# Prompt latent attention with keys on partitions: row maxima as a 97th query feature, no transposes of exponentials

## Chip, cores and metric

One core of one Trainium2 chip. The metric is device time in microseconds (us) of one execution of the whole program; lower is better. The engines are TensorE (PE; its weight loads are listed as PEld), VectorE (DVE), ScalarE (ACT), GpSimd (POOL) and SyncE (SP, which issues the DMAs). L177 is line 177 of the kernel file.

## What is computed

Two layers of a streaming encoder for 1024 prompt tokens and, with the same weights, 32 later sample tokens; model width 1024. In each layer three groups of heads work side by side: retention (4 heads), latent attention (8 heads, in the code `mla`) and a band attention (4 heads). Their outputs, times a gate, are concatenated and projected back. The change touches the prompt's latent attention alone:

```python
def _mla_prompt_attn(q, k, v):          # q, k: 96 features (64 normed + 32 rotated), v: 64
    scale = dq ** -0.5
    key_chunk = jnp.arange(S) // CHUNK   # CHUNK = 64
    def one_block(args):                 # a block of 128 queries
        q_chunk = (b_idx * Q_BLOCK + jnp.arange(Q_BLOCK)) // CHUNK
        s = jnp.einsum('bqhd,bkhd->bhqk', q_blk, k) * scale
        s = jnp.where(key_chunk[None, :] <= q_chunk[:, None], s, NEG_INF)
        p = jax.nn.softmax(s, axis=-1)
        return jnp.einsum('bhqk,bkhd->bqhd', p, v)
mix = jnp.concatenate([ret_o * silu(a_g), mla_o * silu(b_g), band_o * silu(c_g)], -1)
y = x + jnp.einsum('bte,ed->btd', mix, w_out)
```

## The kernel before

All of it is one program, written by the class `Kern`. Tokens are 9 tiles: 8 of 128 prompt tokens and one with the 32 of the sample. A product that needs more precision than the rounded type float32r gives is split in a high and a low part and takes three PE instructions: high times high, high times low, low times high.

`run` (L1526) goes through the layers. `layer_in` (L1431) makes the input projections in steps and spawns tasks: retention, band attention, the sample, and `mla_pair` (L784) for the first pair of heads. `mla_pair` loads queries, keys and values of two heads from DRAM (`sk`, `sq`, `sv`), transposes queries and keys on PE and writes their high and low parts to `self.sets` (in the trace `H`), with the 96 features on partitions.

Then `run` iterates over `mla(l)` (L821), which goes through units: 4 pairs of heads `hp`, 8 query tiles `b`, 2 heads `i` of the pair. A unit has three steps:

- `score` (L825): the scores of 128 queries (on partitions) with the `128 * (b + 1)` keys up to their own tile, in two pieces above 512. Three products a piece, then the masked corner, a row maximum on DVE, and on ACT the exponential, with the negated maximum as its bias and the sum of each row as second output. The exponentials are called `P`.
- `turn`, one unit later (`LAG_T`): `transposed` (L1204) turns each 128x128 block of `P` on PE by a product with the identity, so that keys come to partitions, and copies it out of PSUM (`PT`).
- `value`, two units later (`LAG_V`): for both heads of the pair, `pv` (L863) multiplies each `PT` block with the values of its key tile. Head 0 fills output rows 0 to 63 and head 1 rows 64 to 127: `self.mm(o[64 * i:64 * i + 64], vk[:, 64 * i:64 * i + 64], at[i][k], ...)` (in `values`, L1216). `inverse_rows` (L1231) brings the inverse sums to the features' layout by one more transpose (`rep`), and the result goes into `mix`.

Between the units `run` puts pieces of the output projection `out_part` (L1382), at rates set by `RATES`, `STARTS` and `OUT_PAGES`. The second of its two calls, with feature tiles that hold the latent heads, starts a token tile when `self.full` says that the last pair of heads is done for it; `pv` sets it to `b + 1`.

The order in which Python emits all this comes from the tasks (`poll`, `press`, `drive`, with rough prices per instruction); a scheduler then sets the final order on each engine. PSUM has 8 banks: 3 named `ps`, 3 `s`, 2 `pj`. SBUF has 60 pages of 128x512 float32.

Of the kernel before, what the change touches and what calls it, by code (L numbers as in the profile page):

```python
# [35 lines left out]
RATES = (0.45, 0.4, 0.8)  # L36
SMALL = 4
STARTS = (2, 40)
OUT_PAGES = (14, 20)
# [12 lines left out]
LAG_T, LAG_V = 1, 2  # L52
MLA_ORDER = "stv"
PAIR_AT = 2
# [3 lines left out]
NEED = dict(prep=4, misc=2, b=10, ret=4, bk=2, bq=7, band=12, smp=3, mla=4)  # L58
# [32 lines left out]
class Task:  # L91
    """A foreground task: its pages held, and whether and when it can go on."""
# [6 lines left out]
class Kern:  # L99
# [19 lines left out]
    # ---- storage  # L119
# [44 lines left out]
    # ---- instructions, each with its rough price for the emission order  # L164
# [87 lines left out]
    # ---- order of emission: background products, foreground tasks where they are ready  # L252
# [3 lines left out]
    def safe(self, k, task=None):  # L256
        """Whether the started tasks can still end, one after the other, when k pages are taken (by task)."""
# [65 lines left out]
    # ---- constants  # L323
    def setup(self):
# [4 lines left out]
        nc.vector.memset(self.ones, 1.0)  # L329
        self.nhalf = cp.tile([128, 16], F32, name="nhalf")  # L330
# [14 lines left out]
        self.G = cp.tile([128, 256], F32, name="G")  # L345
# [34 lines left out]
    def load_layer(self, l):  # L380
        A = self.A
        G = A["gains"]
        self.load(self.G, bass.AP(tensor=G.tensor, offset=G.offset + l * 256, ap=[[0, 128], [1, 256]]))
# [3 lines left out]
        self.ts(self.gret, self.cols[:, 2:4], 0.5, None, OP.mult)  # L387
        for j in range(2):
# [3 lines left out]

    def load_bias(self, l):
        """8 (bias - the bias of far keys) of the last 256 keys, masked, rows by query."""
# [87 lines left out]
    def first_prep(self, t, hT):  # L482
        """The first layer takes its input as it is, turned by the layout; its products are scaled by the rows' norms."""
# [40 lines left out]
    # ---- products of all tokens with one chunk of columns  # L524
# [19 lines left out]
    def stacked(self, p, ws, fts=range(8)):  # L544
        """Sample rows: high parts' products on rows 0-31, low parts' on 32-63 (64-95 only fill the array)."""
# [5 lines left out]
    def unload(self, t, p, W, z=None):  # L551
        """A chunk's product of token tile t in SBUF."""
# [13 lines left out]
    # ---- latent attention: queries, keys and values of a token tile  # L566
# [58 lines left out]
    def rope(self, x, cos, sin, tmp, out, H, half, n, eng, first="G"):  # L625
        """x, out: [n, H, 2, half]; tmp as x; cos, sin: [n, half] or [n, 2, half]."""
# [11 lines left out]
    def latent(self, p, ch, cl, ws):  # L638
        """Products of latents; without cl, ch holds high parts in columns 0-31 and low parts in 32-63."""
# [180 lines left out]

    def mla(self, l):  # L821
        sets = self.sets
        P, sums, PT = {}, {}, {}

        def score(hp, i, b):  # L825
            hs = sets[(2 * hp + i) % 4]
            nk = 128 * (b + 1)
            if nk <= 512:
                halves = [(0, nk)]
            else:  # L830
                a = 128 * ((b + 2) // 2)
                halves = [(0, a), (a, nk)]
            q = slice(128 * b, 128 * b + 128)
            m = self.st(2)
            pss = []
            for j, (a, e) in enumerate(halves):
                s = self.bank((e - a,), "pj" if self.spare and (j if len(halves) == 2 else i) else "s")
                self.mm(s, hs[:96, 2, q], hs[:96, 0, a:e], True, False)
                self.mm(s, hs[:96, 2, q], hs[:96, 1, a:e], False, False)
                self.mm(s, hs[:96, 3, q], hs[:96, 0, a:e], False, True)  # L840
                if e == nk:
                    self.memset(s[0:64, e - a - 64:e - a], NEG)
                self.red(m[:, j:j + 1], s, OP.max, negate=True)
                pss.append(s)
            bias = self.st(1)
            if len(halves) == 2:
                self.ts(bias, m[:, 0:1], m[:, 1:2], MLA_SCALE, OP.min, OP.mult)
            else:
                self.ts(bias, m[:, 0:1], MLA_SCALE, None, OP.mult)
            if not i:  # L850
# [800 lines left out]
```

## Time and profile before

| | |
|---|---|
| three runs | 1393.87, 1394.78 (median), 1399.46 us |
| profiled execution, span | 1392.4 us, 28787 instructions |
| PE busy | 1357.6 us (98%) |
| DVE busy | 864.9 us (62%) |
| ACT busy | 765.8 us (55%) |
| POOL busy | 457.8 us (33%) |
| DMA | 130.57 MB, mean 94 GB/s |

The profiled execution has no other time of its own than its span; the median of the three runs is 2.4 us above it. Busy time of PE is from instructions that overlap each other, since matmuls are pipelined. "a <- b" in a row of instructions is output from inputs; in a row of waits it is the waiting instruction and what released it.

### The profile page before, as it was taken

How to read it: one execution, taken by the hardware profiler on the slowest of the kernel's cores; microseconds unless marked ns; L12 is line 12 of the kernel's file. 1: busy time of each engine (PE TensorE's matmuls, PEld its weight loads, DVE VectorE, ACT ScalarE, POOL GpSimd, SP SyncE). 2: the span in 40 equal slices, each digit the busy share in tenths (PEclk: the TensorE clock that was granted, in tenths of full speed). 3: DMA queues.
4: the chain of work that ended last, by engine and by line, in shares of the span. 5: the costliest groups of instructions: out<-in, count | busy, mean ns of one | idle time of the engine just before them, and what ended most of it. 6: DMA issues, size and time to landing. Idle time of an engine off the chain costs nothing.

```text
span 1392.4 us, 28787 instructions
## 1 busy us (share of the span) xinstructions
PE 1357.6 (98%) x10339; PEld 1222.2 (88%) x10339; DVE 864.9 (62%) x2745; ACT 765.8 (55%) x2190; POOL 457.8 (33%) x682
## 2 busy tenths in 40 slices
PE   6899999999999999999999999999999999999998
PEld 6899998999998788888889999999989988788886
DVE  7655667567677556666563555675766675657553
ACT  6545544354556656676662444453645575657641
POOL 4555776243000313221222556654410021313110
PEclk9999999999999999999999999999999999999999
DMA  6334331121112333423330344311112132433231
GB/s 235 108 91 155 112 113 30 54 84 45 55 47 76 107 116 109 161 75 107 110 126 30 109 130 134 102 35 58 58 35 77 46 98 94 144 118 118 75 106 72
DMA packets 131078, 130.57 MB, mean 94 GB/s; under 512 B 14392, under 2 KB 107256, under 8 KB 130936
## 3 DMA queue, kind: packets, MB, share of 16 engines
q1 hardware_dynamic: 130936, 128.74, 29.6%
q8 instruction: 82, 1.34, 0.4%
q14 instruction: 60, 0.49, 0.1%
HBM read 84.48 MB, written 45.79 MB: 94 GB/s over the span
## 4 chain that ended last, share of the span: by engine, by line
PE 83%; DMA 7%; POOL 3%; DVE 2%; ACT 2%; issue 1%; SPq 1%; ACTq 0%; DVEq 0%; POOLq 0%
PE pj L177 47%; PE ps L177 12%; PE s L177 11%; PE ps L183 9%; DMA raw<-in_w_in 2%; PE pj L183 2%; POOL rs L242 2%; PE s L183 1%; DMA bt<-in_bflip 1%; SPq L247 1%; DMA sk<-kd 1%; DMA braw<-bt 1%; DMA raw<-in_w_out 1%; POOL ms L203 1%; DVE st L214 1%
## 5 line engine op out<-in xcount | busy, mean ns | idle before, releaser
L177 PE MATMUL pj<-whi,H 128*128 128x256 f32 (+1 forms) x1792 | 368.4, 298 | 12.2 <-DVE whi L203 7.4
L177 PEld LDWEIGHTS pj<-whi,H 128*128 128x128 f32 x1792 | 295.4, 192 | 16.8 <-ACT xt L187 7.3
L177 PE MATMUL pj<-wlo,H 128*128 128x256 f32 (+1 forms) x896 | 265.6, 297 | 1.3 <-DVE wlo L210 1.3
L195 POOL TENSOR_TENSOR mlo<-mix,mhi 128x256 fp32r<-128x256 f32 x96 | 69.0, 736 | 493.0 <-ACT mhi L187 183.8
L177 PE MATMUL pj<-H,whi 128*128 128x256 f32 (+1 forms) x1024 | 206.5, 295 | 0.0
L187 ACT ACTIVATE PT<-ps 128x384 f32<-128x384 f32 (+3 forms) x304 | 131.0, 455 | 129.6 <-PE ps L183 127.2
L177 PEld LDWEIGHTS pj<-wlo,H 128*128 128x128 f32 x896 | 172.0, 192 | 3.6 <-DVE wlo L210 2.2
L242 POOL TENSOR_TENSOR rs<-ms,nhalf 128x4 f32<-128x4 f32 (+5 forms) x141 | 164.8, 1169 | 9.4
L177 PEld LDWEIGHTS pj<-H,whi 128*128 128x128 f32 x1024 | 164.0, 193 | 2.6 <-issue 1.5
L177 PE MATMUL pj<-H,wlo 128*128 128x256 f32 (+1 forms) x512 | 150.0, 293 | 0.0
L203 POOL TENSOR_SCALAR ms<-st 128x4 f32<-128x4 f32 (+6 forms) x166 | 57.3, 345 | 243.1 <-DVE st L214 214.7
L177 PE MATMUL s<-H 96*128 96x384 f32 (+2 forms) x522 | 127.4, 363 | 0.4 <-ACT P L187 0.4
L214 DVE TENSOR_REDUCE st<-s 128x1 f32<-128x384 f32 (+3 forms) x222 | 118.5, 536 | 6.7 <-PE s L177 4.6
L187 ACT ACTIVATE whi<-raw,cols 128x256 fp32r<-128x256 f32 (+2 forms) x178 | 83.1, 515 | 71.0 <-DMA raw<-in_w_in 60.2
L210 DVE SCALAR_TENSOR_TENSOR wlo<-raw,cols,whi 128x256 fp32r<-128x256 f32 (+2 forms) x184 | 89.6, 520 | 42.8 <-ACT whi L187 41.4
L187 ACT ACTIVATE P<-s,st 128x384 f32<-128x384 f32 (+2 forms) x174 | 100.2, 582 | 21.3 <-DVE st L203 20.5
L177 PE MATMUL pj<-whi,mhi 128*128 128x512 f32 x256 | 103.9, 406 | 0.3 <-ACT P L187 0.2
L177 PE MATMUL pj<-wlo,mhi 128*128 128x512 f32 x256 | 101.4, 396 | 0.0
L177 PE MATMUL pj<-whi,mlo 128*128 128x512 f32 x256 | 101.3, 397 | 0.0
L177 PEld LDWEIGHTS pj<-H,wlo 128*128 128x128 f32 x512 | 98.6, 193 | 0.8 <-issue 0.5
L177 PEld LDWEIGHTS s<-H 96*128 96x128 f32 x522 | 84.2, 191 | 9.1 <-issue 1.7
L183 PE MATMUL ps<-ident,P 128*128 128x128 f32 x576 | 87.1, 274 | 2.2 <-ACT PT L187 1.4
(260 smaller groups left out, 2844.3 us busy)
## 6 DMA issues: line engine op xcount, KB each, us to landing
raw<-in_w_in SPq DMA_DIRECT2D x80, 256.0 KB, 3.0
raw<-in_w_out SPq DMA_DIRECT2D x32, 256.0 KB, 2.7
yp<-yres SPq DMA_DIRECT2D x32, 256.0 KB, 2.6
yres<-yp SPq DMA_DIRECT2D x32, 256.0 KB, 2.7
qd<-qn SPq DMA_DIRECT2D x32, 192.0 KB, 1.9
kd<-kt SPq DMA_DIRECT2D x32, 192.0 KB, 2.1
sk<-kd SPq DMA_DIRECT2D x32, 192.0 KB, 3.1
sq<-qd SPq DMA_DIRECT2D x32, 192.0 KB, 2.5
```

The costliest lines, as they stand in the source:

```text
L177: self.nc.tensor.matmul(out, lhsT, rhs, start=start, stop=stop)
L183: self.nc.tensor.transpose(out, in_, self.ident[:k, :k])
L187: r = self.nc.scalar.activation(out, in_, func, **kw)
L195: (self.nc.vector if eng == "D" else self.nc.gpsimd).tensor_tensor(out, a, b, op=op)
L203: (self.nc.vector if eng == "D" else self.nc.gpsimd).tensor_scalar(out, a, s1, s2, op0=op0, **kw)
L210: self.nc.vector.scalar_tensor_tensor(out, a, s, b, op0=op0, op1=op1)
L214: self.nc.vector.tensor_reduce(out, in_, axis=AX.X, op=op, negate=negate)
L242: self.nc.gpsimd.tensor_tensor(r[:n], ms[:n], self.nhalf[:n, :w], op=OP.pow)
L247: self.nc.sync.dma_start(dst, src)
```

## The change

In the latent attention of the prompt the scores are made with keys on partitions. A unit is now a key tile `j` of 128 keys and one half `Q` of the queries: 512 queries, or those from the key tile's own start on. Their exponentials are what the product with the values takes, so no exponential is transposed. As a row maximum can't be a bias there (queries lie along the free axis), it comes in through the product: the high parts of queries and keys get a 97th row, which holds 1 for each key and the negated maximum for each query. The maxima come from a pass before, `mla_max`, with the high parts alone and queries on partitions: one product for each piece, DVE maxima, four PE transposes for each half, an ACT copy for each head. `mla_ahead` does this for a pair of heads ahead of its scores. `score_margin` works out per layer, from the gains, a constant bias that covers the error of maxima from high parts. Sums of exponentials: POOL adds the exponentials of all key tiles (`acc`), and one PE product with a column block of twos sums over partitions. The inverse goes through two DVE transposes by blocks of 32. Value products are emitted in groups of four key tiles (`GROUP`), and `self.full` is set once for each half. Some constants of the emission order change as well.

```diff
-RATES = (0.45, 0.4, 0.8)
-SMALL = 4
-STARTS = (2, 40)
-OUT_PAGES = (14, 20)
+RATES = (0.23, 0.5)
+STARTS = (2, 60)
+OUT_PAGES, GO_PAGES = (16, 22), 8
-LAG_T, LAG_V = 1, 2
-MLA_ORDER = "stv"
-PAIR_AT = 2
+LAG_V, GROUP = 3, 4
-NEED = dict(prep=4, misc=2, b=10, ret=4, bk=2, bq=7, band=12, smp=3, mla=4)
+NEED = dict(prep=4, misc=2, b=10, ret=4, bk=2, bq=7, band=12, smp=3, mla=7)
...
+        self.twos = cp.tile([128, 64], F32, name="twos")
+        nc.vector.memset(self.twos, 2.0)
...
+    def score_margin(self):
...
+        a = self.st(4)
+        for j, (c, e) in enumerate(((256, 320), (224, 256), (320, 384), (128, 160))):
+            self.nc.vector.tensor_reduce(a[:, j:j + 1], self.G[:, c:e], axis=AX.X, op=OP.max, apply_absolute_value=True)
...
+    def mla_keep(self, hp):
+        for i in range(2):
+            hs = self.sets[(2 * hp + i) % 4]
+            self.memset(hs[96:97, 0].bitcast(F32), 1.0, "G")
...
+    def mla_max(self, l, hp):
+        for half in range(2):
+            mt = self.page([65, 4], name="mt")
+            self.memset(mt, 0.0, "G")
+            for b in range(4 * half, 4 * half + 4):
...
+                    for j, (a, e) in enumerate(halves):
+                        s = self.bank((e - a,), "o")
+                        self.mm(s, hs[:96, 2, q], hs[:96, 0, a:e], True, True)
+                        if e == nk:
+                            self.memset(s[0:64, e - a - 64:e - a], NEG)
+                        self.red(m[:, j:j + 1], s, OP.max, negate=True)
...
+            p = self.bank((4, 128), "o")
+            for b in range(4):
+                self.tr(p[:65, b], mt[:, :, b])
...
+                self.act(hs[96:97, 2, 512 * half:512 * half + 512], p[64 * i:64 * i + 1].rearrange("p a b -> p (a b)"))
...
+        def score(x):
+            hp, Q, j, i = units[x]
             hs = sets[(2 * hp + i) % 4]
...
+            a, e = max(512 * Q, 128 * j), 512 * Q + 512
...
+            self.mm(s, hs[:97, 0, k], hs[:97, 2, q], True, False)
+            self.mm(s, hs[:96, 0, k], hs[:96, 3, q], False, False)
+            self.mm(s, hs[:96, 1, k], hs[:96, 2, q], False, True)
+            if a == 128 * j:
+                self.memset(s[64:128, 0:64], NEG)
+            t = self.page([e - a], name="PT")
+            self.act(t, s, AF.Exp, scale=MLA_SCALE, bias=self.mbias)
...
+                self.tt(acc[hp, Q, i][:, c:], acc[hp, Q, i][:, c:], t, OP.add, eng="G")
+
+        def value(hp, Q, js):
...
+            for j in js:
+                c = max(0, 128 * j - 512 * Q)
+                for i in range(2):
+                    t = PT.pop((hp, Q, j, i))
+                    v = self.vals[hp][j // 4][:, j % 4, 64 * i:64 * i + 64]
+                    self.mm(o[64 * i:64 * i + 64, c:], v, t, j == 0, j == last)
+                    self.free(t)
...
+                self.mm(sm[64 * i:64 * i + 64], self.twos, acc[hp, Q, i], True, True)
...
+            self.nc.vector.transpose(u, sm)
+            r = self.st(16)
+            self.recip(r, u.rearrange("p (a b) -> p a b", b=32)[:, :, 0])
+            w = self.page([512], name="inv")
+            self.nc.vector.transpose(w.rearrange("p (a b) -> p a b", b=32), r.unsqueeze(2).to_broadcast([128, 16, 32]))
...
+            self.tt(w, o, w, OP.mult)
...
             if hp == 3:
-                self.full = b + 1
+                self.full = 4 * Q + 4
```

**Order, first place: PE, the products of exponentials with values.** Names: `P` exponentials, `PT` exponentials with keys on partitions, `sv` values, `mt` maxima, `acc` added exponentials, `H_94` and so on the queries and keys of one head. Before, second layer:

```order
L183 MATMUL ps_18760<-ident,P_18700 128x128 x4
L177 MATMUL ps_18767<-PT_18675,sv_18052 64x128
L177 MATMUL pj_19135<-H_94 128x512 x3
L177 MATMUL ps_18767<-PT_18717,sv_18052 64x128
L177 MATMUL ps_18767<-PT_18675,sv_18052 64x128
...
L183 MATMUL ps_18778<-ident,rep_18776 128x128
L177 MATMUL s_18951<-H_94 128x384 x3
```

The same work now, first layer:

```order
L174 MATMUL ps_7537<-PT_7479,sv_6526 64x512
L174 MATMUL ps_7537<-PT_7496,sv_6526 64x512
L174 MATMUL ps_7537<-PT_7534,sv_6526 64x384
L174 MATMUL ps_7537<-PT_7551,sv_6526 64x384
L174 MATMUL ps_7537<-PT_7559,sv_6526 64x256
L174 MATMUL ps_7537<-PT_7567,sv_6526 64x256
L174 MATMUL ps_7537<-PT_7598,sv_6526 64x128
L180 MATMUL ps_7499<-ident,mt_7358 65x128
L174 MATMUL ps_7537<-PT_7606,sv_6526 64x128
L174 MATMUL ps_7681<-acc_7316,twos 64x512
L174 MATMUL ps_7681<-acc_7349,twos 64x512
L174 MATMUL s_7784<-H_97 128x128 x3
```

The transposes of `P` and `rep` are gone, value products have up to 512 columns and stand two heads in turn, and behind a half stand the two products of its sums.

**Second place: PE, the last heads of the first layer now.** Here value products stand between scores:

```order
L174 MATMUL s_8961<-H_98 128x512 x3
L174 MATMUL ps_9146<-PT_8924,sv_8329 64x512
L174 MATMUL s_8969<-H_97 128x512 x3
L174 MATMUL ps_9146<-PT_8930,sv_8329 64x512
L174 MATMUL s_9011<-H_98 128x512 x3
L174 MATMUL ps_9146<-PT_8936,sv_8329 64x512
L174 MATMUL s_9018<-H_97 128x512 x3
L174 MATMUL ps_9146<-PT_8965,sv_8329 64x512
```

Each of these value products has a score of the same stretch on both sides, instead of its fellow of the other head.

**Third place: PE, the end of the second layer.** `mhi` and `mlo` are the parts of the mixed outputs, `whi` and `wlo` those of the output weights. Before, the last value products and the output tiles behind them:

```order
L177 MATMUL ps_19988<-PT_19934,sv_18812 64x128
L177 MATMUL ps_19988<-PT_19986,sv_18812 64x128
L177 MATMUL pj_20078<-wlo_18860,mhi_20026 128x512
L177 MATMUL pj_20078<-whi_18859,mlo_20027 128x512
L177 MATMUL pj_20078<-whi_18865,mhi_20026 128x512
...
L177 MATMUL pj_20093<-whi_18823,mhi_20066 128x512
```

Now, the last product of sums and what follows (seven rows of the same kind are left out):

```order
L174 MATMUL ps_18466<-acc_18225,twos 64x512
L174 MATMUL pj_18503<-whi_17829,mlo_18408 128x512
L174 MATMUL pj_18518<-whi_17787,mhi_18491 128x512
L174 MATMUL pj_18518<-wlo_17788,mhi_18491 128x512
L174 MATMUL pj_18518<-whi_17787,mlo_18492 128x512
...
L174 MATMUL pj_18543<-wlo_17818,mhi_18491 128x512
L174 MATMUL pj_18543<-whi_17817,mlo_18492 128x512
L174 MATMUL pj_18518<-whi_17799,mhi_18491 128x512
```

Behind the last sums there are thirteen products of output tiles whose features don't come from the last pair of heads; the row after them, with `whi_17799`, takes features that do.

## Rows read from the trace of the kernel before

**Rows 1.** The page's first part: span, and busy time of each engine.

```profile
span 1392.4 us, 28787 instructions
...
PE 1357.6 (98%) x10339; PEld 1222.2 (88%) x10339; DVE 864.9 (62%) x2745; ACT 765.8 (55%) x2190; POOL 457.8 (33%) x682
```

**Rows 2.** Stretches: start:end and length, busy us of each engine, PEclk.

```profile
430.00:460.00 30.00, 25.78 (x213) 20.89 (x212) 19.55 (x84) 21.17 (x68) 6.13 (x7) 0.97 0.33 102
...
470.00:705.00 235.00, 233.82 (x1710) 194.16 (x1709) 150.41 (x463) 155.49 (x417) 52.36 (x75) 1.00 0.35 113
...
1130.00:1150.00 20.00, 18.88 (x151) 16.02 (x150) 15.98 (x60) 16.97 (x54) 7.85 (x8) 1.00 0.44 139
```

**Rows 3.** PE's waits in 470 to 705, then in 430 to 470 us.

```profile
PE pj L183 <- DMA sk<-kd: 0.8, 1, 0.8
PE pj L177 <- ACT P L187: 0.2, 1, 0.2
...
PE ps L183 <- ACT bPA L187: 1.5, 2, 0.9
```

**Rows 4.** PE's timeline in five stretches: start, length of the group, instruction.

```profile
462.67 0.39 PE L177 MATMUL pj<-whi,mhi 128*128 128x512 f32 x1
462.99 0.43 PE L177 MATMUL ps<-PT,sv 128*64 128x128 f32 x2
463.35 0.33 PE L183 MATMUL ps<-ident,rep 128*128 128x128 f32 x1
...
470.74 0.60 PE L183 MATMUL pj<-ident,sk 128*96 128x128 f32 x4
471.17 0.27 PE L183 MATMUL ps<-ident,rep 128*128 128x128 f32 x1
471.20 0.60 PE L177 MATMUL s<-H 96*128 96x256 f32 x3
471.73 0.65 PE L177 MATMUL ps<-PT,sv 128*64 128x128 f32 x6
...
501.30 1.31 PE L177 MATMUL ps<-PT,sv 128*64 128x128 f32 x20
502.54 0.50 PE L177 MATMUL pj<-whi,mlo 128*128 128x512 f32 x1
...
503.11 0.40 PE L177 MATMUL pj<-wlo,mhi 128*128 128x512 f32 x1
...
503.81 0.39 PE L177 MATMUL pj<-wlo,mhi 128*128 128x512 f32 x1
...
531.07 0.44 PE L177 MATMUL ps<-PT,sv 128*64 128x128 f32 x4
531.44 0.33 PE L183 MATMUL ps<-ident,rep 128*128 128x128 f32 x1
...
539.01 0.69 PE L177 MATMUL s<-H 96*128 96x384 f32 x3
539.54 0.60 PE L183 MATMUL ps<-ident,P 128*128 128x128 f32 x4
```

**Rows 5.** Groups by form, whole span: instruction, count, busy us, mean ns.

```profile
L195 POOL TENSOR_TENSOR wlo<-raw,whi 128x512 fp32r<-128x512 f32 x32 | 40.7, 1281 | 64.1 <-ACT whi L187 57.2 <-PE s L177 5.2 <-PE ps L183 1.3
L195 POOL TENSOR_TENSOR mlo<-mix,mhi 128x256 fp32r<-128x256 f32 x96 | 69.0, 736 | 493.0 <-ACT mhi L187 183.8 <-DVE s L226 95.4 <-DVE mix L195 95.2
...
L195 DVE TENSOR_TENSOR yres<-pj,yres 128x512 f32<-128x512 f32 x64 | 44.1, 691 | 46.9 <-PE pj L177 45.8 <-issue 0.3
L222 DVE RECIPROCAL st<-sums 128x2 f32<-128x2 f32 x64 | 9.9, 154 | 0.1
L195 DVE TENSOR_TENSOR mix<-mix,th 128x256 f32<-128x256 f32 x20 | 8.7, 436 | 0.2
L214 DVE TENSOR_REDUCE xsq<-xt 128x128 f32<-128x512 f32 x8 | 8.6, 1071 | 3.2 <-POOL xt L195 3.2
...
L187 ACT ACTIVATE mhi<-mix 128x256 fp32r<-128x256 f32 x96 | 36.7, 415 | 17.8 <-DVE mix L195 10.4 <-PE ps L183 3.5 <-DMA yp<-yres 2.6
```

More of the change, by code (lines that the diff above doesn't have):

```diff
@@ L821, in mla, with mla_ahead @@
+    def mla_ahead(self, l, hp):
+        if hp < 2:
+            self.mla_keep(hp)
+        yield from self.mla_pair(l, hp)
+        yield from self.mla_max(l, hp)
     def mla(self, l):
         sets = self.sets
-        P, sums, PT = {}, {}, {}
-        def score(hp, i, b):
+        PT, acc, first, outs = {}, {}, {}, {}
+        def score(x):
+            hp, Q, j, i = units[x]
             hs = sets[(2 * hp + i) % 4]
-            nk = 128 * (b + 1)
-            if nk <= 512:
-                halves = [(0, nk)]
-            else:
[L831 to L850, printed above, removed]
-                sums[hp, b] = self.st(2, "sums")
-            so = sums[hp, b][:, i:i + 1]
-            sm = self.st(2) if len(halves) == 2 else so
-            pg = []
-            for j, (a, e) in enumerate(halves):
-                t = self.page([e - a], name="P")
-                self.act(t, pss[j], AF.Exp, scale=MLA_SCALE, bias=bias, accum_out=sm[:, j:j + 1])
-                pg.append((a // 128, e // 128, t))
-            if len(halves) == 2:
-                self.tt(so, sm[:, 0:1], sm[:, 1:2], OP.add)
-            P[hp, i, b] = pg
@@ L863, in pv @@
-        def pv(hp, b):
-            o = self.bank((128,), "o")
-            self.values(o, [(k, self.vals[hp][k // 4][:, k % 4]) for k in range(b + 1)],
-                        [PT.pop((hp, i, b)) for i in range(2)])
-            mx = self.mixat(2 + hp, b)
-            self.put_mix((2 + hp,), (b,), mx, self.inverse_rows(sums.pop((hp, b))))
-            self.tt(mx, o, mx, OP.mult)
+            a, e = max(512 * Q, 128 * j), 512 * Q + 512
+            c = a - 512 * Q
+            k, q = slice(128 * j, 128 * j + 128), slice(a, e)
@@ new lines, in score @@
+            if j == 0:
+                first[i] = t
+            elif j == 1:
+                acc[hp, Q, i] = self.page([512], name="acc")
+                u = first.pop(i)
+                if c:
+                    self.nc.gpsimd.tensor_copy(acc[hp, Q, i][:, :c], u[:, :c])
+                    self.tick("G", 300)
+                self.tt(acc[hp, Q, i][:, c:], u[:, c:], t, OP.add, eng="G")
+            else:
+                self.tt(acc[hp, Q, i][:, c:], acc[hp, Q, i][:, c:], t, OP.add, eng="G")
@@ L870, in pv @@
             if hp == 3:
-                self.full = b + 1
-            if b == 7:
+                self.full = 4 * Q + 4
+            if Q:
                 self.free(*self.vals[hp])
-        units = [(hp, i, b) for hp in range(4) for b in range(8) for i in range(2)]
-        nxt = None
-        n = len(units)
-        def scores(x):
-            nonlocal nxt
-            if x < n:
-                score(*units[x])
-                self.scored = x == n - 1
-                if x % 16 == PAIR_AT and x < 48:
-                    nxt = self.mla_pair(l, units[x][0] + 1)
-                if nxt is not None:
-                    next(nxt, None)
@@ L888, in turn @@
-        def turn(x):
-            x -= LAG_T
-            if 0 <= x < n:
-                PT[units[x]] = self.transposed(P.pop(units[x]))
-        def value(x):
-            x -= LAG_V
-            if 0 <= x < n and units[x][1]:
-                pv(units[x][0], units[x][2])
-        do = dict(s=scores, t=turn, v=value)
-        for x in range(n + LAG_V):
-            with self.urgent(URGENT_MLA):
-                for step in MLA_ORDER:
-                    do[step](x)
+        units = [(hp, Q, j, i) for hp in range(4) for Q in range(2) for j in range(4 * Q + 4) for i in range(2)]
@@ new lines, in mla @@
+        groups = {}
+        for x, (hp, Q, j, i) in enumerate(units):
+            if i and j % GROUP == GROUP - 1:
+                groups[x + LAG_V] = hp, Q, range(j - GROUP + 1, j + 1)
+        n = len(units)
+        nxt = None
+        for x in range(n + LAG_V + 1):
+            with self.urgent(URGENT_MLA):
+                if x < n:
+                    hp = units[x][0]
+                    if x == 0 or units[x - 1][0] != hp:
+                        for _ in nxt or ():
+                            pass
+                        nxt = self.mla_ahead(l, hp + 1) if hp < 3 else None
+                    score(x)
+                    self.scored = x == n - 1
+                    if nxt is not None:
+                        for _ in range(1 + (x % 2)):
+                            next(nxt, None)
+                if x in groups:
+                    value(*groups[x])
@@ L1425, in out_part @@
                 self.free(*(ys[c] for c in cs))
-            if halves and x == 7:
+            if halves and x == 8:
                 weights((1,))
@@ L1483, in gen @@
             return self.chunk(self.W.pop(name), 416 if name == "b" else 256, hT, cbs[name])
-        self.spawn("mla", self.mla_pair(l, 0), lambda: self.turns >= 4 and not self.bleft)
+        self.spawn("mla", self.mla_ahead(l, 0), lambda: self.turns >= 4 and not self.bleft)
         for name, nxt in zip(STEPS, STEPS[1:] + (None,)):
```

52 lines of the change are left out of this document (47 added, 5 removed).

## Prediction

> **What bounds the kernel now.** I read the page first: TensorE is busy 98% of a span of 1392.4 us, every other engine 62% or less [rows 1]. A share over the whole span could still hide a stretch with another limit, so the stretches came next [rows 2]. The change touches the latent attention of the prompt, which fills 430 to 705 us in the first layer and 1130 us to the end in the second. In 470 to 705 us PE is busy for 233.82 of 235.00 us. Who released PE there is a short list: 0.8 us for a DMA and 0.2 us for ACT [rows 3]. In this stage, then, time is what PE's instructions take one behind the other; work taken from ACT and DVE (155.49 and 150.41 of 235 us busy) buys nothing by itself. Only the entry to the stage has idle PE: 25.78 of 30 us are busy in 430 to 460 us, with ACT named as releaser [rows 2, 3].
>
> Busy sums cannot price a matmul, since each overlaps the next. The price is the distance from start to start in a full stretch of the timeline [rows 4]:
> - 512 columns, rounded type: 503.11 to 503.81 us is three steps, 0.233 us each. 384 columns: three in 539.01 to 539.54, 0.177 each.
> - A transpose of 128 columns: four in 470.74 to 471.17, 0.108 each.
> - 256 columns: from 471.17 to 471.73 stand one transpose, three products and the entry to the next kind (0.09, below): 0.56 - 0.11 - 0.09 leaves 0.12 each. I use 0.12 for 128 columns too.
> - Exponentials times values (float32, 64 output rows, one head in each half of the array; the profile counts each product twice): one product alone takes 462.99 to 463.35, 0.36 us; two, one of each head, 531.07 to 531.44, 0.37 us. So two heads run side by side, and **a product without its partner costs as much as the pair**. Ten products take 501.30 to 502.54, 1.24 us: four more pairs in 0.87, 0.217 a pair. What is left, 0.37 - 0.217 = 0.15, is paid once at the end of such a run, and 0.09 at its start (462.67 to 462.99 is 0.32 in place of 0.233): **0.24 us a run**.
>
> **The change part by part, on PE** (16 heads: 8 in each of 2 layers).
>
> Taken out. Score products of each head before: 1 piece of 128 keys, 2 of 256, 5 of 384, 4 of 512, three products each. That is 144 x 0.12 + 240 x 0.177 + 192 x 0.233 = 104.5 us. Transposes of exponentials, 36 a head: 576 x 0.108 = 62.2. Transposes of the inverse sums: 64 x 0.108 = 6.9. Products with values: 288 pairs x 0.217 = 62.5, and 3.7 more for 11 products that stand alone and odd ends in the printed order. Together 239.8 us.
>
> Put in. The same columns of scores, now in 2 pieces each of 128, 256 and 384 and 6 of 512 queries a head: 192 x 0.12 + 96 x 0.177 + 288 x 0.233 = 107.1. The pass for the maxima, one product for each old piece: 48 x 0.12 + 80 x 0.177 + 64 x 0.233 = 34.9. Transposes of the maxima: 64 x 0.108 = 6.9. Values: 288 pairs' worth of columns again, 62.5. Sums through the column of twos: 16 pairs of 512 columns at 4 x 0.217 = 0.87, 13.9. And the products that lost their partner: with the last heads of a layer the order puts single value products between scores (second piece of the order). Over both layers I count alone 16 of 512 columns, 7 of 384, 6 of 256, 5 of 128 and 3 sums, and odd ends of longer runs. At half a pair's price each that is +16.5. Together 241.8 us.
>
> So PE's own work rises by 2.0 us. Runs of the two-heads kind fall from 165 to 143 in the whole program: -22 x 0.24 = -5.3. **PE net: -3.3 us.** The 62 us of transposes are spent again on maxima, sums and lost partners.
>
> A product of 512 columns with 64 output rows does not occur before. If its halves still run side by side, 0.87 a pair; if not, 1.74, and values and sums cost 62.5 + 13.9 = 76 us more. I take 0.87, since pair and single agree to 0.01 us at 128 columns and nothing in the rows depends on the length.
>
> **Off PE.** ACT loses 576 columns-blocks of copies and the reads of sums, DVE its two-column work; both were hidden and stay so: nothing. POOL gets 16 copies and 160 additions. By the nearest rows 512 columns take 1.28 us and 256 take 0.74 [rows 5], so some 155 us in both layers. POOL has room, 52.36 of 235 us busy [rows 2]: nothing, unless late (rival 2). The margin at each layer's start is 10 DVE instructions of a few tenths on one partition column, beside weight work: at most 2 us, taken as 0. The wider gains load: 0.
>
> **Entry.** The first pair's maxima (34.9 / 8 + 0.9 = 5.2 us of PE) now stand among the last band pieces, where PE idles: 4.2 us in 430 to 460 and, by the row of the second layer, 1.1 us in 1130 to 1150 [rows 2]. They fill part, but the first score also waits for maxima, transpose and ACT's copy into row 96. Gain between 0 and 5.3; I take **-3**.
>
> **Tail of each layer.** Before, tile 7's output follows the last query tile alone. Now output tiles 4 to 7 all wait for the last half's sums: the third piece of the order has 13 products behind the last sum before the first that needs it, 13 x 0.233 = 3.0 us of cover. The chain behind it: two DVE transposes of 128x512, a reciprocal (0.15 for a small one), the product (0.69), gate (0.44), ACT's high part (0.42) [rows 5]. The transposes are not in this trace; the nearest rows for 128x512 on DVE are 0.69 and 1.07, of which I take the first, a plain read of PSUM. 3.1 us, and with six hand-overs between engines (single waits on ACT or DVE last 0.2 to 0.9 us [rows 3]; I take 0.2 to 0.3 each, an estimate) 4.5 to 5. So 1.5 to 3 us a layer, with the longer transposes up to 3.7; I take **+4** for both.
>
> The Trainium skill (VectorE: DVE Perf Modes, The three transpose paths) gives 311 ns for a DVE transpose of 128x128 in bf16. By that, times four, 1.24 us would stand for 0.69 and the sum would be 2.2 us higher; no run here shows it.
>
> **Sum.** -3.3 - 3 + 4 = -2.3 us. The span is 1392.4 us and the median of three runs 1394.78, 2.4 us around it, which I leave as they are: **1392 us**, no change (a run of this kernel can tell about 0.5%, 7 us, from nothing).
>
> **Rivals.**
> 1. *The shorter chain pays.* Score, maximum, exponential, transpose, copy, product becomes score, exponential, product. Priced by the steps above, the stretch 470 to 705 comes to about 227 us, so 8 us there and 7 in the second layer are short waits too small for the list of waits. If half go and the entry fills, 1394.8 - 3.3 - 5.3 - 7.5 + 2 = 1381. For it: ACT and DVE get lighter. Against: the list shows only 1 us, and the missing time may be the matmuls' own. 0.30.
> 2. *Sums late: POOL becomes the bound.* PE reaches the products with the added exponentials in order, and behind them stand the next scores. From the end of one first half's additions to the end of the second half's, in the third pair of heads, POOL has 8 additions of 512, 8 weight parts, 6 low parts and 6 narrow additions: 16 x 1.28 + 8 x 0.74 + 2 x 1.0 + 2 x 0.5 = 29.3 us. PE has 25 us there, and 20 more since that half's first score. It decides from POOL instructions 1.4 times as long as those rows, or where it stands still for weights as long. Then 2 to 4 us at each of the 8 second halves: 1394.8 - 2 + 24 = 1417. The Trainium skill (SBUF — State Buffer, section SBUF: two separate sides) says that a GpSimd read and a DVE instruction with two SBUF inputs shut each other out for a whole instruction. The 736 ns of the low parts, beside a DVE that is busy two thirds of the time, show none of it so far. 0.12.
> 3. *Maxima in front of scores.* Each half's maxima go DVE, PE, ACT into row 96; where the order has no cover, 1 us at each of 16 places: 1408. 0.07. Halves that don't run side by side: 1470. 0.03.
>
> **How the numbers follow.** The forecast has 0.48, with 1386 to 1400 as its own range. Rival 1 is faster (0.30), rivals 2 and 3 slower (0.22); a little of the forecast lies below 1388: faster 0.32, no change 0.46, slower 0.22. The range for 8 in 10 takes in rival 1 with all its short waits (1376) and rival 2 at half price and 3 (1412).
>
> **What would show it.** Right: PE busy over 97% and value products of 512 columns 0.43 us apart by passes, two heads starting together; some 68 runs of this kind in the stage; PE's wait in front of the output tiles once a layer, on DVE or ACT. Wrong: waits of PE on POOL's additions (rival 2), on ACT's copy into row 96 (rival 3), a start distance of single value products well under 0.87 (lost partners cost less), or a stretch in the middle of the stage with clearly more idle PE than 1 us.

## The result, and the profile after

The changed kernel takes 1469.24 us (median of four runs, 1464.23 to 1475.17) against 1397.12 us (1393.87 to 1401.83): ratio 1.0524, 95% interval 1.0495 to 1.0553. It is slower by 72 us. The forecast was 1392 us, the range ended at 1412. The one rival at the right number, 1470 for value products whose halves don't run side by side, is right for a wrong reason, as the rows of the timeline below show.

The first part of the page, for [rows 1]:

```profile
span 1471.3 us, 26417 instructions
...
PE 1393.9 (95%) x9251; PEld 1176.7 (80%) x9251; DVE 861.3 (59%) x2602; ACT 700.4 (48%) x1838; POOL 627.5 (43%) x882
```

ACT lost 65 us, POOL gained 170, and neither is the bound. What counts is span less PE busy: 77.4 us idle, 34.8 before. The stretches, for [rows 2] (start:end, length, busy us of PE, PEld, DVE, ACT and POOL, granted clock, DMA), cut at the last gate product, the first and the last score of each layer:

```profile
441.00:473.00 32.00, 25.51 (x222) 20.96 (x220) 23.61 (x94) 19.80 (x59) 4.81 (x7) 0.93 0.26 74
473.00:707.00 234.00, 221.64 (x1031) 150.39 (x1029) 129.43 (x352) 109.12 (x215) 126.28 (x148) 0.95 0.31 96
...
1166.00:1194.00 28.00, 22.68 (x161) 17.64 (x160) 18.63 (x74) 17.04 (x48) 4.86 (x7) 0.88 0.31 87
1194.00:1432.00 238.00, 224.26 (x1014) 148.40 (x1015) 123.88 (x335) 99.77 (x195) 126.81 (x148) 0.96 0.30 94
```

Before, the same cuts of the stage itself (439 to 684 and 1135 to 1358 us) read:

```profile
439.00:684.00 245.00, 239.60 (x1726) 196.97 (x1726) 154.58 (x510) 161.71 (x449) 55.81 (x72) 0.99 0.34 110
...
1135.00:1358.00 223.00, 221.00 (x1612) 182.05 (x1612) 137.84 (x461) 140.18 (x394) 52.58 (x62) 1.00 0.34 111
```

Two things moved. From the last gate product to the first score pass 32 and 28 us, 5 and 2 before. And inside the stage PE is idle for 12.4 and 13.7 us, 5.4 and 2.0 before, at a granted clock of 0.95 and 0.96. The mean clock of the whole run fell from 0.991 to 0.973. TensorE has two levels, 2.4 and 1.2 GHz, so 0.973 means 2 x 0.027 x 1471 = 79 us at 1.2 GHz, against 2 x 0.009 x 1392 = 25 before. By the trace's clock records PE is busy for 70 us of the time at 1.2 GHz, 24 before. Its products stand nearly twice as far apart there (0.43 us in place of 0.233, below), so about half of that is what the clock costs: 35 us, 12 before.

So of 79 us between the two spans, 43 are idle PE and 23 the clock. The other 13 are PE's own work. Added up over the traces from start to start, with idle time taken out and time at 1.2 GHz counted half, it is 1345 us before and 1358 now. The work that the change doesn't touch takes 1076 us in both.

Who released PE in the stage of the second layer (1166 to 1432 us), for [rows 3]: engine and line that waits, releaser, total us, times, longest.

```profile
PE ps L174 <- DVE st L211: 5.1, 8, 3.2
PE ps L174 <- ACT H L184: 2.0, 2, 1.6
PE ps L174 <- ACT PT L184: 1.8, 2, 1.1
PE s L174 <- ACT H L184: 1.8, 2, 1.1
PE s L174 <- ACT PT L184: 1.3, 3, 0.7
PE pj L180 <- DMA sk<-kd: 1.2, 1, 1.2
```

`DVE st L211` is a maximum, `ACT H L184` the copy of maxima into row 96 and the release of their bank: the pass for the maxima stands first. In the first layer's stage (473 to 707 us) maxima and copies hold PE for 4.6 us, waits for exponentials for 3.1 and loads for 2.7.

### The profile page after: what moved, and what is told of

It reads as the page before. It is cut to its first block, busy times and chain, and to the rows that moved or that the text cites. A ratio compares the mean times of both kernels' runs of the same rounds, so it can differ in the third digit from the quotient of the medians.

```text
span 1471.3 us, 26417 instructions
## 1 busy us (share of the span) xinstructions
PE 1393.9 (95%) x9251; PEld 1176.7 (80%) x9251; DVE 861.3 (59%) x2602; ACT 700.4 (48%) x1838; POOL 627.5 (43%) x882
## 4 chain that ended last, share of the span: by engine, by line
PE 77%; DMA 8%; DVE 6%; ACT 3%; POOL 3%; issue 2%; SPq 1%; DVEq 0%; ACTq 0%; POOLq 0%
PE pj L174 44%; PE ps L174 14%; PE s L174 11%; PE ps L180 4%; DVE st L211 2%; DMA raw<-in_w_in 2%; POOL rs L239 1%; PE pj L180 1%; PE s L180 1%; DMA sk<-kd 1%; DMA raw<-in_w_uq 1%; ACT whi L184 1%; DMA raw<-in_w_out 1%; ACT H L184 1%; DMA braw<-bt 1%
## 5 line engine op out<-in xcount | busy, mean ns | idle before, releaser
L174 PE MATMUL pj<-whi,H 128*128 128x256 f32 (+1 forms) x1792 | 371.3, 299 | 20.1 <-ACT z L184 10.4
L184 ACT ACTIVATE PT<-s,mbias 128x512 f32<-128x512 f32 (+3 forms) x189 | 106.1, 579 | 134.3 <-DVE s L223 61.0
L174 PE MATMUL s<-H 97*128 97x512 f32 (+3 forms) x567 | 140.4, 370 | 6.5 <-ACT PT L184 4.3
L192 POOL TENSOR_TENSOR acc<-acc,PT 128x512 f32<-128x512 f32 (+3 forms) x128 | 117.7, 932 | 52.3 <-ACT PT L184 49.6
L174 PEld LDWEIGHTS s<-H 97*128 97x128 f32 x567 | 97.8, 199 | 45.3 <-ACT PT L184 23.2
L184 ACT ACTIVATE whi<-raw,cols 128x256 fp32r<-128x256 f32 (+2 forms) x178 | 83.5, 514 | 83.1 <-DMA raw<-in_w_in 56.6
L174 PE MATMUL ps<-PT,sv 128*64 128x512 f32 (+3 forms) x384 | 92.0, 516 | 0.3
L192 DVE TENSOR_TENSOR yres<-pj,yres 128x512 f32<-128x512 f32 (+1 forms) x72 | 49.5, 687 | 72.5 <-PE pj L174 71.3
```

The costliest lines, as they stand in the source:

```text
L174: self.nc.tensor.matmul(out, lhsT, rhs, start=start, stop=stop)
L184: r = self.nc.scalar.activation(out, in_, func, **kw)
L192: (self.nc.vector if eng == "D" else self.nc.gpsimd).tensor_tensor(out, a, b, op=op)
```

## The longest wait, engine by engine

PE's timeline at that 3.2 us wait (start, length, instruction, idle before and releaser):

```profile
1349.72 0.62 PE L174 MATMUL s<-H 97*128 97x256 f32 x3
1353.55 1.48 PE L174 MATMUL ps<-H 96*128 96x384 f32 x2 [3.21 <-DVE st L211]
1354.83 0.84 PE L174 MATMUL s<-H 97*128 97x256 f32 x3
1355.47 0.63 PE L174 MATMUL pj<-whi,mlo 128*128 128x512 f32 x1
1355.90 0.63 PE L174 MATMUL pj<-whi,mhi 128*128 128x512 f32 x1
```

DVE in the same microseconds:

```profile
1348.54 0.56 DVE L211 TENSOR_REDUCE st<-ps 128x1 f32<-128x384 f32 x1 [0.80 <-PE ps L174]
1349.02 4.15 DVE L192 TENSOR_TENSOR mix<-inv,mix 128x256 f32<-128x256 f32 x2
1353.09 0.41 DVE L211 TENSOR_REDUCE st<-ps 128x1 f32<-128x256 f32 x1
```

And POOL:

```profile
1348.67 1.29 POOL L192 TENSOR_TENSOR acc<-acc,PT 128x512 f32<-128x512 f32 x1
1349.92 1.41 POOL L192 TENSOR_TENSOR mlo<-mix,mhi 128x256 fp32r<-128x256 f32 x2
1351.29 1.26 POOL L192 TENSOR_TENSOR acc<-acc,PT 128x512 f32<-128x512 f32 x1
1353.30 1.27 POOL L192 TENSOR_TENSOR wlo<-raw,whi 128x512 fp32r<-128x512 f32 x1 [0.75 <-issue]
```

Two products of 128x256 take 4.15 us. Their records show that it is the first that is held: it runs from 1349.02 to 1352.83, 3.81 us, and the second takes 0.41. In that time POOL runs two additions with two low parts between them, four instructions without a gap, and the held product ends 0.28 us after the last of them. The next maximum stands behind them on DVE, its bank is not read, PE has none for the next product of the pass and waits. From 1355.47 on PE's products of 512 columns are 0.43 us apart in place of 0.233: the clock of 1350 to 1360 us is 0.66. So one wait is paid twice. The Trainium skill (SBUF — State Buffer, SBUF: two separate sides) has the rule: a DVE instruction with two SBUF inputs and a GpSimd one that reads SBUF exclude each other for a whole instruction. The trace agrees, and here DVE did not get in between the four. The prediction looked for it in POOL's rows and found none; it stands in DVE's. Over the whole run the groups by form show it, for [rows 5]:

```profile
L192 DVE TENSOR_TENSOR mix<-inv,mix 128x256 f32<-128x256 f32 x32 | 23.4, 770 | 0.2
L192 DVE TENSOR_TENSOR mt<-st 128x1 f32<-128x1 f32 x64 | 16.0, 250 | 0.5
L192 DVE TENSOR_TENSOR mix<-mix,th 128x256 f32<-128x256 f32 x20 | 8.7, 435 | 0.2
L930 DVE STREAM_TRANSPOSE sumT<-ps 128x512 f32<-128x512 f32 x16 | 11.5, 716 | 63.7 <-PE ps L174 59.1 <-POOL mlo L192 4.4
L934 DVE STREAM_TRANSPOSE inv<-st 128x512 f32<-128x512 f32 x16 | 11.3, 704 | 0.7
```

The first and the third row are the same shape; the third is from the gates, before the stage. The mean of 770 ns mixes 20 products of 0.40 to 0.43 us with 12 of 0.48 to 3.81.

## The experiments

All ratios are to the kernel before, run on the same chip, with 95% intervals. In e2, e3, e9 and e16 exponentials are taken of a hundredth of the scores, so these four don't compute the attention of the reference. "PE's own work" and the cost of the clock are counted from the traces as in the result.

**First four: what the waits belong to.**

e1_margin, against the changed kernel (`score_margin` in `mla_ahead`, for the first pair):

```diff
-        self.score_margin()   # in load_layer
...
+        if not hp:
+            self.score_margin()
```

> The margin of the scores is worked out when the first pair of heads is turned, not at the start of the layer. Theory start: in the changed kernel the first 40 us hold PE waits of 4.4 and 3.3 us for ACT's z that before did not have, and 6.8 us more at half clock; with the margin away from there the first 437 us come back by 6 to 8 us, span about 1464. Rival: these waits belong to the new order of everything, not to the margin; then no change within 3 us.

Measured 1.0438 (1.0319 to 1.0556), 1453.98 us. In 20 to 50 us PE is busy for 23.99 us at clock 0.94; in the changed kernel 18.88 at 0.77, before 24.09 at 0.89. The second layer's first product of 416 columns comes at 745.3 us, not 752.1. The start theory holds, with 7 us in the first layer by the trace; the interval of the whole time is too wide to show it.

e2_noadd, against the changed kernel:

```diff
-            else:
-                self.tt(acc[hp, Q, i][:, c:], acc[hp, Q, i][:, c:], t, OP.add, eng="G")
```

> POOL's additions from the third key tile on are left out, and exponentials are taken of a hundredth of the scores, so that sums stay finite; outputs of the attention are not those of the reference. Theory port (a two-input DVE instruction on SBUF waits while POOL's additions run, and PE waits behind it with the clock falling): the gating products on DVE fall from 770 to about 440 ns, the two longest waits on DVE maxima (1.3 and 3.2 us) go, and the span falls by 10 to 25 us, to 1446 to 1461. Theory structure (maxima, bank by bank, hold PE whatever POOL does): within 5 us of 1471. Theory lone products: no change either.

Measured 1.0443 (1.0392 to 1.0494), 1454.75 us, 11 us less than the changed kernel by the ratio. The longest wait for a maximum is 0.7 us, not 3.2; the gating products take 647 ns, not 440, with POOL still making low parts. So additions cost PE something, but over four fifths of the loss remain without them. The mean clock is 0.976 in both executions, inside the changed kernel's 0.970 to 0.979, so exponentials of a hundredth of the scores do not give the clock back by themselves.

e3_nomax, against the changed kernel:

```diff
-        yield from self.mla_max(l, hp)
```

> The pass for the maxima is left out (row 96 of the queries stays 0, exponentials of a hundredth of the scores). Its PE work by start distances is 34.9 + 6.9 = 42 us. Theory structure (the pass brings waits and low clock beyond its own work): the span falls by 60 to 80 us, to 1391 to 1411, and PE's idle time of 77 us falls by 20 or more. Rival (the pass costs its PE work alone): 1425 to 1435, idle as before.

Measured 1.0162 (1.0093 to 1.0231), 1415.57 us. From the first to the last score of the first layer PE waits for this and nothing else:

```profile
PE pj L180 <- PE ps L174: 0.6, 1, 0.6
PE pj L174 <- DVE H L207: 0.2, 1, 0.2
```

The span, busy times, and that stretch (columns as for [rows 2]):

```profile
span 1416.6 us, 25437 instructions
...
PE 1378.6 (97%) x8995; PEld 1125.0 (79%) x8995; DVE 747.0 (53%) x2218; ACT 679.3 (48%) x1806; POOL 627.0 (44%) x874
...
455.00:682.00 227.00, 226.02 (x1010) 133.95 (x1009) 85.16 (x206) 108.42 (x227) 128.24 (x147) 1.00 0.32 104
```

Idle PE falls from 77 to 38 us, and what the clock costs from 35 to 14. That is 61 of the 66 us by which the two together had grown over the kernel before, so the rival (the pass costs its PE work alone) is out. The profiled span is 6 us above the theory's range because something else grew. With the pass gone its 58 us of PE's own work go too, but by the trace 129 value products and sums stand alone, 37 before. Value products and sums take 149 us in place of 102, and scores 131 in place of 119.

e4_dveadd has `eng="G"` taken off the two additions.

> The additions of exponentials run on DVE, not on POOL. Theory port: DVE has two-input work without POOL beside it, gating products near 440 ns; DVE gets some 80 to 100 us more over both layers; span 1455 to 1475. Theory structure: DVE is in the way of PE already, with the additions in its queue the waits on maxima grow, 1480 to 1510.

Measured 1.0591 (1.0536 to 1.0646), 1475.32 us: gating products at 520 ns, no gain. DVE is busy for 63 us more in all, so what it wins by POOL's silence it seems to spend on the additions.

**Next four, on e1_margin: what would shorten the waits.**

e5_fill: `RATES = (0.23, 0.5)` becomes `(0.3, 0.3)`.

> On the kernel with the margin moved (1454 us), the output projection is emitted at rates 0.3 and 0.3 in place of 0.23 and 0.5: more of it early in the stage, less late. Theory filler (PE waits because the order holds too little other work beside the maxima): waits and half clock shrink in the first half of the stage, 1435 to 1447. Theory maxima (each wait comes from a DVE maximum, whatever stands around): 1448 to 1460.

Measured 1.0343 (1.0271 to 1.0415), 1437.52 us, 13 us under e1_margin by the ratio, with overlapping intervals. The number is the filler theory's, its reason only in part. Idle PE falls by 9 us, but the mean clock does not rise (0.974 and 0.970, e1_margin 0.977 and 0.984). PE's own work falls by some 20 us: the new order leaves 17 value products and sums alone in place of 39, and has 51 runs of them in place of 70. That is the gain that e8 aims at, and this run does not tell it from the filler's.

e6_port:

```diff
-                        self.tt(at, m[:, 0:1], m[:, 1:2], OP.min)
+                        self.ts(at, m[:, 0:1], m[:, 1:2], None, OP.min)
...
-            self.tt(m, src, m, OP.mult)
+            self.tt(m, src, m, OP.mult, eng="G" if src.shape[-1] == 256 else "D")
```

> With the margin moved, DVE has no two-input instruction on SBUF in the new code: the minimum of two maxima takes one as a scalar operand, and the gating product of 256 columns runs on POOL. All arithmetic stays. Theory port: the 1.3 and 3.2 us waits on maxima behind the gating products go, with the half clock behind them; 1440 to 1448. Rival (the additions left out won 17 us in another way, through a lighter POOL): no gain or a loss, 1452 to 1462, as POOL gets 24 us of gating.

Measured 1.0430 (1.0397 to 1.0463), 1449.62 us. Waits for maxima fall from 8.0 to 3.3 us, the longest to 1.0, and idle PE in the profiled executions from 67 to 57, yet the ratio is that of e1_margin, whose interval is 33 us wide. The exclusion of DVE and POOL is real; whether its end is worth nothing or some 10 us, this run does not show. It is not the size of the loss.

e7_spread: `for _ in range(1 + (x % 2))` around the pass becomes one step a unit.

> With the margin moved, the pass for the next pair is emitted one step a unit in place of one and a half, so its maxima stand among longer scores. Theory maxima too dense: idle PE in the stage falls by a third, 1440 to 1450. Rival (what waits is the hand-over at the turn of the pairs, where the last steps now come at once): 1452 to 1465.

Measured 1.0490 (1.0442 to 1.0538), 1457.97 us, inside e1_margin's interval: no gain.

e8_pairs:

```diff
+                    with self.urgent(300 * i):
                         self.mm(o[64 * i:64 * i + 64, c:], v, t, j == 0, j == last)
```

> With the margin moved, the value product of the second head gets priority in the order, so that fewer products stand alone: by the printed order single ones hold 7040 columns in place of 15104. At 4 cycles a column and 2.4 GHz half of the pair's price is saved: 8064 x 0.83 ns = 6.7 us. Theory lone products: 1445 to 1450. Rival (PE then waits as much longer elsewhere): 1452 to 1456.

Measured 1.0391 (1.0356 to 1.0426), 1444.23 us: 7 us by the ratio, as priced, though e1_margin's interval is too wide to show it by itself. The trace has 22 value products alone with 7040 columns, as forecast, and 10 us less of PE's own work.

**Then the maxima by themselves, and the edits together.**

e9_shortmax, on e1_margin: `self.red(m[:, j:j + 1], s, ...)` reads `s[:, :32]`.

> On the kernel with the margin moved (1454 us, ratio 1.044), DVE takes the maxima of the pass over 32 keys of each piece in place of 128 to 512 (exponentials of a hundredth of the scores, outputs of the attention not those of the reference); all PE products of the pass stay. DVE loses about 192 x 0.45 = 86 us over both layers. Theory DVE time (PE waits for banks until DVE has read them): ratio 1.015 to 1.03, waits on DVE maxima near 0, half clock below 50 us. Theory hand-overs (what counts is the number of turns between PE, DVE and ACT): ratio 1.035 to 1.045.

Measured 1.0249 (1.0170 to 1.0328), 1428.79 us, the DVE theory: DVE lost 53 us of busy time (the shorter maxima still take 0.18 us), PE all its products kept, and the time fell by 25 us. The two intervals just touch; e16 repeats the step with clear ones.

e10_all holds the edits of e1, e5, e6 and e8.

> The four edits together, all arithmetic kept: margin moved, second head's value products first, no two-input SBUF instruction on DVE in the new code, output projection at rates 0.3 and 0.3. If their gains add (margin 14, pairs 7, filler 13, port 0 to 4), the ratio to before is 1.025 or a little less. If filler and pairs win the same waits, 1.03 to 1.035. Below 1.00 is expected by neither.

Measured 1.0154 (1.0102 to 1.0205), 1415.51 us: a larger gain than the four together, which come to 1.029. In this order 9 value products stand alone, fewer than in e5 or e8.

e11_early: `self.turns >= 4` becomes `>= 1`. The sets of the heads lie in the storage of the layer's input, which the last gates still read, so the gates here are worked out from other values; the instructions are the same.

> As the four edits together, and the first pair of heads with its maxima may start after one turn of the last gates in place of four. Theory entry (from the last gate products to the first score 33 and 28 us pass, 4.5 and 2 before, for want of other work beside the first pair's maxima): this stretch shrinks by 5 to 10 us a layer and the time by as much, ratio 0.01 under the four edits. Rival (the band attention, whose exponentials stand before the maxima on ACT and DVE, sets it): no change.

Measured 1.0170 (1.0117 to 1.0222), 1417.77 us: no change, but not for the rival's reason. The entry did shrink: from the last gate product to the first score 19 us pass in the first layer, 37 in e10_all (16 and 24 in the second). Some of the waits now stand behind the first score. PE in 420 to 510 us, which holds the same number of products in both, e10_all first (columns as for [rows 2]):

```profile
420.00:510.00 90.00, 80.39 (x561) 66.47 (x560) 60.04 (x207) 49.58 (x127) 24.89 (x32) 0.94 0.28 89
420.00:510.00 90.00, 81.72 (x561) 67.78 (x561) 57.07 (x214) 50.64 (x131) 26.20 (x33) 0.92 0.23 71
```

So the length of the entry is not a loss in itself.

e12_group2: `LAG_V, GROUP = 3, 2` and rates 0.4 and 0.4.

> As the four edits, with value products emitted in groups of two key tiles in place of four, which frees pages of exponentials sooner, and the output projection at rates 0.4 and 0.4. Theory filler (pages held by exponentials keep the output projection back): 5 to 10 us under the four edits. Against it: 65 runs of value products in place of 46 in the order, some 6 us, and 1900 more columns alone, 2 us.

Measured 1.0336 (1.0267 to 1.0404), 1440.86 us, worse by 25 us than e10_all, a miss for the filler. PE idles 10 us longer, waits for maxima grow from 1.8 to 9.1 us, and PE's own work by 13 us, with 65 runs of value products in place of 46. The clock has no part in it in the profiled executions (0.981, e10_all 0.982).

**Last, with loads ahead.**

e13_prefetch, on e10_all, in `mla_pair`:

```diff
         nxt = stage(*turns[0])
+        yield
```

> As the four edits together (ratio 1.015), and the first keys of the next pair are loaded one step ahead of their transposes. Theory loads (PE waits 9.1 us for these loads there): ratio 1.008 to 1.011. Rival (the loads wait for the same pages as before, or the time goes to the next wait): 1.013 to 1.017.

Measured 1.0124 (1.0072 to 1.0175), 1407.95 us. Waits for these loads go from 9.1 to 0.4 us, idle PE in all only from 54 to 52; the interval overlaps e10_all's, so neither theory is shown. This kernel also shows the clock by itself. Four executions of the same instructions in the same order took spans of 1399.6, 1400.6, 1411.7 and 1412.6 us, at mean clocks of 0.990, 0.992, 0.978 and 0.978. The lower clock comes with 12 us.

e14_banks, on e13_prefetch: `self.bank((e - a,), "pj" if i else "o")` for the maxima.

> As e13_prefetch, and the maxima's products of the second head use the two banks of the output projection and of the transposes. Theory banks: waits on DVE maxima go, 3 to 8 us less than e13_prefetch. Rival (the banks are then missing to the output projection, whose products fill the waits): the same or slower by some us; by the order there are also 63 runs of value products in place of 41, about 5 us.

Measured 1.0328 (1.0266 to 1.0390), 1438.52 us, slower, and the banks theory is out: PE's waits for maxima in the pass grow from 0.8 to 6.3 us. The rival's direction is right; the trace has 63 runs of value products in place of 41, and that the output projection misses its banks is argued, not shown.

e15_rate, on e13_prefetch: rates 0.36 and 0.3.

> As e13_prefetch, with the output projection at rates 0.36 and 0.3. Theory filler goes on: 3 to 8 us less. Rival (filler has done what it can): within 3 us.

Measured 1.0237 (1.0196 to 1.0278), 1425.92 us, 18 us slower, which neither expected. Of the rates tried, 0.3 and 0.3 are the best.

e16_short, on e13_prefetch: maxima over 32 keys, as in e9.

> As e13_prefetch, with the maxima taken over 32 keys of a piece (exponentials of a hundredth of the scores; outputs of the attention not those of the reference). Theory DVE time: again 15 to 26 us less, ratio about 0.99 to 1.00. Rival (the four edits have hidden what DVE's maxima cost): less than 8 us.

Measured 0.9925 (0.9888 to 0.9962), 1382.35 us. Two hundredths again, 26 us by the medians. The profile, its span, and the same part of e13_prefetch:

```profile
span 1376.1 us, 26500 instructions
...
PE 1333.4 (97%) x9251; PEld 1154.9 (84%) x9251; DVE 785.5 (57%) x2570; ACT 697.2 (51%) x1838; POOL 645.4 (47%) x914
```

```profile
span 1399.6 us, 26444 instructions
...
PE 1348.0 (96%) x9251; PEld 1160.4 (83%) x9251; DVE 839.1 (60%) x2570; ACT 699.7 (50%) x1838; POOL 646.9 (46%) x914
```

The order has as few value products alone as e13_prefetch (7). The same PE products take 14.6 us less of busy time where DVE is done sooner: about half of that is PE at the lower clock (mean 0.990 and 0.995), and idle PE falls by 9 us besides.

e17_first, on e13_prefetch: the masks and maxima of the pass with `self.urgent(300)`.

> As e13_prefetch, with the masks and maxima of the pass given priority in the order on DVE. Theory queue (they stand behind other DVE work, banks are held meanwhile): 8 to 15 us less than e13_prefetch, ratio 1.000 to 1.006. Rival (their own length, 0.28 to 0.68 us each, is what holds the banks): within 4 us of e13_prefetch, ratio 1.010 to 1.015.

Measured 1.0097 (1.0062 to 1.0131), 1403.26 us, the number of both rival and no change at all. The trace has the instructions of PE, DVE, ACT and POOL in the order of e13_prefetch, one by one, so the priority changed nothing, and the run does not test whether the maxima stand in a queue. Read as one kernel, e13 and e17 are the fastest version that computes everything, 4% under the changed kernel and 1.0 to 1.2% above the one before. No version that computes everything is faster than the kernel before.

## Why the prediction was wrong, step by step

The step that failed is a wait that the sum put at nothing. Work off PE was "nothing", and maxima in front of scores were rival 3, 16 us at 0.07. The pass makes PE wait for DVE and ACT, and the clock falls with the waits: 66 us more than before, of which 61 go when the pass is left out (e3). A smaller error is in PE's own work, 13 us up where 3.3 down was forecast.

**"PE net: -3.3 us".** The prices of value products hold. Value products of 512 columns, one of each head, and one product alone, in the changed kernel:

```profile
660.08 1.08 PE L174 MATMUL ps<-PT,sv 128*64 128x512 f32 x4
661.09 0.62 PE L174 MATMUL s<-H 97*128 97x256 f32 x3
...
673.33 1.07 PE L174 MATMUL ps<-PT,sv 128*64 128x512 f32 x2
674.33 0.97 PE L174 MATMUL s<-H 97*128 97x512 f32 x3
```

1.01 us for the pair and 1.00 for the single: side by side, 0.86 and the end of the run, so the rival at 1470 is out, and a lost partner costs what was said. e8 moves as this price says. The net is 13 us and not -3.3. Nearly all of the difference is in the pass: it takes 48.6 us where 34.9 were counted, and its transposes 9.5 where 6.9 were. The 34.9 is the price in a row of equal products, but these stand one, two or three at a time among others, in 126 groups. At the 0.09 us that the prediction found for the entry to another kind, that is an estimated 11 of the 14 us. Part of the 48.6 is waits too short for the list, since with shorter maxima the same products take 43.9 (e16).

**"Entry: -3".** This failed. The pass of the first pair was to fill idle PE. From the last gate product to the first score 32 and 28 us pass now, 16.5 and 10.4 without the pass (e3): it delays the first score by 16 to 17 us a layer for 5.2 us of products. PE idles for 6.5 and 5.3 us of these stretches, at clocks of 0.93 and 0.88; in e3 for 1.5 and 0.4, at 1.00. So the pass brought some 10 us of idle PE where 3 were to be gained. The list of waits there names a load (1.9 us), the band attention's work on DVE and ACT, which the maxima share, and one maximum (0.4 us). The delay by itself is not the loss: in e11 it is 18 us shorter in the first layer, and the kernel no faster.

**"At most 2 us, taken as 0" for the margin.** 7 us in the first layer by the trace. Ten small instructions put DVE's order at the start another way, and PE waits 4.4 and 3.3 us for ACT's z, where products of the first projection then run at half clock.

**Rival 3, "1 us at each of 16 places", 0.07.** The right mechanism, several times too small (16 us against 61) and not only there. Each of the 192 products of the pass, not each half, holds a bank until DVE has read it, 0.28 to 0.68 us a maximum, with DVE's other work ahead. e9 and e16 measure DVE's part of it, 25 and 26 us with every PE product in place; e3 shows that with the pass gone PE waits for less than 1 us in each stage. And the sum had no term for the clock: every idle stretch was taken at its own length.

**Off PE, "both were hidden and stay so: nothing".** This came from reading DVE as a share, two thirds busy. Before, DVE took maxima too, but three products of a score stood on PE for each of them, with transposes between; the pass has one. DVE had room and was late nevertheless.

**Rival 1, the shorter chain, 0.30.** Nothing in the traces speaks for it: idle PE grew in both stages.

**Rival 2, POOL's sums.** POOL's additions took 1.30 us for 512 columns, as said, and were not late. At the end of the first layer the last one ends at 708.5 us and PE asks for the sums at 714.2. What the traces show of POOL's cost goes by way of DVE.

**"Tail: +4".** The chain is as priced: DVE transposes 0.72 and 0.70 us, the high part at 719.1 after sums that end at 715.3. PE waited 0.8 us for it in the second layer and not at all in the first, so less than said. The Trainium skill (VectorE: DVE Perf Modes, The three transpose paths) led to an estimate of 1.24 us, which this shape does not bear out.

What stays open: how the waits of the entry divide between DVE and ACT; how much of the maxima's cost is their own length and how much DVE's other work ahead of them, since e17 left the order as it was; and how much of e5's gain is the filler's.

## What to carry to other kernels

A cheap product that another engine must read before the next may start is priced by that engine: per bank, DVE's time for the maximum, not PE's for the product. On a PE that is 98% busy, ask of each new hand-over what stands beside it to fill the gap, and pay for the gap at half clock behind it as well. When an experiment changes constants or priorities of a scheduler, compare the order of the instructions before reading its time: e5 also changed how many products stood alone, and e17 changed nothing.

## What the runs showed of the hardware

- One DVE product of 128x256 with both inputs in SBUF, 0.40 to 0.43 us in 20 of 32 cases, took 3.81 us beside four POOL instructions without a gap between them; the mean over 32 was 0.77 us, 0.52 with POOL's additions moved to DVE.
- One order of instructions, eight executions (e13 and e17): spans of 1397 to 1401 us at mean clocks of 0.990 to 0.994, 1404 and 1405 at 0.987, 1412 and 1413 at 0.978.
- A float32 product of 512 columns on half of the array takes 1.00 us to the next start, two of them, one on each half, 1.01.
- A DVE transpose of 128x512 float32 in blocks of 32 takes 0.70 to 0.72 us.
